# A two-layer decoder trunk: the up products of the experts as one product of 512 columns

## The chip, the core and the metric

One core of a Trainium2 chip runs the kernel, one launch for the whole trunk. The metric is the device time of that launch in microseconds (us), the median of several runs. Nothing is shared with other cores.

## The reference

The trunk has two layers. Each mixes 256 tokens of 1024 features with four token mixers; then layer 0 has a dense SwiGLU and layer 1 the part that matters here, eight SwiGLU experts of which each token takes its best two:

```python
def moe_swiglu(h, router_w, w1, w3, w2):
    logits = (xt @ router_w)
    top_v, top_i = lax.top_k(logits, TOP_K)
    gate = jax.nn.softmax(top_v, axis=-1)
    ...
    a = lax.ragged_dot(xs, w1, sizes)
    g = lax.ragged_dot(xs, w3, sizes)
    y = lax.ragged_dot(jax.nn.silu(a) * g, w2, sizes)
    y = y * gate.reshape(-1)[order][:, None]
    return jnp.zeros_like(xt).at[tok].add(y)
```

All is float32. w1 and w3 have 1024 rows and 2816 columns for each expert, w2 has 2816 rows and 1024 columns. Each expert's three matrices are read once, 277 MB in all.

## The kernel before, in words

**Products.** TensorE holds one operand, the stationary one (128 x 128, loaded by a weight load), and streams the other, the moving one, through it. A float32 product is made of three passes over halves that add up to the operands: `mm3` (line 642) issues xh times wh, xh times wl, and xl times wh into the same sums in PSUM. In the experts the tokens are stationary and the weights move.

**Weights.** `Stream` (line 138) loads weight pieces of 1 MB (128 partitions x 2048 columns) from a plan, in order, into a ring of slots; SyncE issues a load as soon as a slot is free. Each piece is split in two halves of 1024 columns: ScalarE writes the high part `wh` (a copy to the rounded type), VectorE the low part `wl` (raw minus wh), and the second half's split gives the slot back. The split halves live in a ring of four buffers (`NWH`, line 587), so a split can begin when the products of the half four places before it are done. `halves` (line 258) gives out a piece's halves and asks ahead of each for the splits of the next three.

**The experts' loop.** `moe` (line 1626) first routes, and gathers each expert's tokens into 128 slots. Then it goes over `pairs`, 8 experts x 11 chunks of 256 of the 2816 columns: 88 steps, in the loop from line 1841. Before the change a step i is, in the order of the code:

- `u`: 24 products of 256 columns (8 k tiles of the 1024 features x 3 passes) of the chunk of w1, by `up_half` (line 1810), into a PSUM bank of the pool `psm`, which has two; ScalarE's Silu of it goes to `es`;
- `at`: two transposes of the `es` of step i-1 (`flip_act`, line 1820), which ScalarE and VectorE split into `ath` (both halves under this name);
- `v`: the same 24 products of the chunk of w3, into the other bank; VectorE multiplies `es` by it;
- at some steps four products `scm` that scatter a finished expert's output to the tokens, or the turning of a one-hot (`rtm`);
- `y`: 12 products of 512 columns (`down`, line 1831) of step i-1 with its piece of w2, into two banks that sum over the expert's 11 chunks;
- at some steps four products `g` that gather tokens for the next two experts.

Six split halves are used in a step, two by each of u, v and y. For experts 3 and 7 the tokens lie in a tile `xe`, for the others in halves of `hh` and `hl`; the names in the rows say which.

**What sets the order.** Each engine runs its instructions in the order of the code. Splits come where `halves` asks for them, so a Silu's place among ScalarE's splits follows from where the code writes it. All instructions go through a helper, so that every row of the profile bears its line, L385; the tile names tell them apart.

Of the kernel before, what the change touches and what calls it, by code (L numbers as in the profile page):

```python
"""Two decoder layers (adaLN, four token mixers, SwiGLU / top-2 experts) in one launch.

Activations live feature-major ([feature on partitions, token on the free axis]) so that
weights are the stationary operand and no result of the dense layers needs a transpose.
Float32 products run as three float32r passes over exact two-way splits of both operands
(x = xh + xl, w = wh + wl): xh*wh + xl*wh + xh*wl.
"""
# [16 lines left out]
OP = mybir.AluOpType  # L24
# [18 lines left out]
# adaLN segments (layer, which) whose products run beside the mixers and the dense SwiGLU, and the  # L43
# least distance of their chunks
# [10 lines left out]
# products that nobody reads, at the places of the start where the tensor engine would wait  # L55
# [41 lines left out]
# the columns kept from the start on, those that the mixers use (the first of them at once), those of the experts  # L97
# [40 lines left out]
class Stream:  # L138
    """Weight chunks, loaded ahead in the plan's order through a ring of slots and split in two when
    they have come (the first two chunks' halves in turn); other chunks go on request through slots  # L140
    of their own."""
# [22 lines left out]
    def add_slots(self, pool, names, last=None):  # L164
        """last: key of the last chunk that may use these slots (None: no limit)."""
        for n in names:
            self.limit[n] = len(self.plan) if last is None else self.index[last]
            self.free.append((pool, n))
        self.issue()

    def add_halves(self, pool, names, last=None):
        """Buffers for split halves, used in turn."""
        for n in names:
            self.limit["wh" + n] = len(self.plan) if last is None else self.index[last]
            self.wring.appendleft((pool, n))
            self.look += 1

    def lane(self, name):
        """(chunks asked for, free slots) of a lane beside the ring."""
        return self.lanes.setdefault(name, (deque(), deque()))  # L180
# [5 lines left out]
    def move(self, lane, last=None):  # L186
        """A lane's slots, all free by now, go to the ring."""
# [39 lines left out]
    def ensure(self, upto):  # L227
        """Emit the splits of the pieces before this one."""
# [40 lines left out]
    def came(self, key):  # L269
        """When an unsplit chunk is there."""  # L270
# [10 lines left out]
class Clock:  # L281
    """A rough time per engine, kept as instructions are emitted: each starts when its engine is free
    and the operands (their boxes in a tile, the tile that had the buffer before) are."""
# [25 lines left out]
    def tile(self, ap):  # L309
        """The tile's accesses so far, {(box, engine, write): end}; those of the buffer's last owner  # L310
        count as one."""
# [14 lines left out]
    def free_at(self, tag, bufs):  # L326
        """When the next buffer of a tag is free."""
# [45 lines left out]
class Timed:  # L373
    """An engine whose instructions go through the clock."""
# [26 lines left out]
class Weave:  # L401
    """Emits the steps of background threads between the products of the main stream, so that no
    in-order engine gets a step whose inputs come late.

    A thread yields None after a step, "sync" before one that begins with a product of what the last
    step made, or a condition that gives False or the time it came true."""
# [65 lines left out]
class Ring:  # L472
    """Buffers handed out in turn: one is free again when all handed out before it are. The names in
    seq take theirs in that order, which keeps the threads from locking each other out."""
# [23 lines left out]
def trunk(ctx, tc, A):  # L498
# [28 lines left out]
    # ---------------------------------------------------------------- plan of the weight stream  # L527
# [12 lines left out]
    def add_item(it):  # L540
# [13 lines left out]
        elif k in ("e1", "e3"):  # L554
            add(it, A["moe_w1" if k == "e1" else "moe_w3"][0, l, it[2]])
# [22 lines left out]
    moe_items = with_lag([(("e1", e, j), ("e3", e, j)) for e, j in pairs], [("e2", e, j) for e, j in pairs])  # L578
# [11 lines left out]
    # ---------------------------------------------------------------- small loads  # L590
# [42 lines left out]
    # ---------------------------------------------------------------- helpers  # L633
# [8 lines left out]
    def mm3(out, ah, al, bh, bl, start, stop):  # L642
        """out += a^T b with a (stationary) and b (moving) both split.

        start clears the written marks of the whole bank, so where a bank holds several sums that
        grow side by side only its first product starts and only its last stops."""
# [4 lines left out]
    # ---------------------------------------------------------------- adaLN vectors  # L651
# [6 lines left out]
    def ada_mm(out, w, kk, start, stop):  # L658
        """One k tile of a segment: four column groups of 256, each on its own 32 rows."""
# [18 lines left out]
    def warm(n):  # L678
        """Products that nobody reads, where the tensor engine would wait: its clock halves when it idles."""
# [8 lines left out]
    def ada_cols(q, fill=lambda: warm(WARM[0])):  # L688
        """Two feature tiles of the two segments that the start waits for; fill puts other products where
        the tensor engine waits."""  # L690
# [18 lines left out]
    def ada_thread(ls, step):  # L709
        """The same products beside other work, a chunk per step of the clock: on DVE, but for the last sum."""  # L710
# [35 lines left out]
    class Gap:  # L746
        """A segment's products that fill the tensor engine's waits around a norm."""
# [30 lines left out]
    # ---------------------------------------------------------------- rope tables  # L778
# [25 lines left out]
    # ---------------------------------------------------------------- norm + modulation  # L804
# [3 lines left out]
    class Norm:  # L808
        """Sums of squares gathered as the features of x become final, then h = split(norm(x))."""
# [5 lines left out]
        def feed(self, dp):  # L815
            """Squares of feature tiles 2 dp, 2 dp + 1; those of the first two pairs are added up."""
# [14 lines left out]
        def feed_all(self):  # L831
            """The same for all of x at once, added up beforehand."""
# [13 lines left out]
        def stats(self, fill=lambda: None):  # L846
            """1 / rms on every partition, by token; fill puts other products where the tensor engine waits."""
# [20 lines left out]
        def tiles(self, ds, l, which, each=None):  # L868
            """Feature tiles ds of h; each(d): work that follows tile d."""
# [34 lines left out]
    # ---------------------------------------------------------------- dense products  # L904
    def feat_part(ps, w, h, ks):
        """ps[:, t*256 + tok] += (h W)[feature, tok] for a chunk's two feature tiles: k tiles ks of half h."""
# [7 lines left out]
    def tok_part(ps, w, h, ks, n=256):  # L914
        """ps[:, i*256 + c] += (h W)[token, column c] of token tile i."""
# [19 lines left out]
    def acc_chunk(key, ps4, xh, xl, first, then=None, mid=None):  # L935
        """ps4[d//2][:, (d%2)*256 + tok] += sum over the chunk's two k tiles (one per half).

        then: this is the last chunk, its pairs of feature tiles are finished one after the other and
        then(pair) takes them up."""
# [19 lines left out]
    # ---------------------------------------------------------------- mixer  # L959
    def mixer(l, mb, mp, pre):  # L960
        """pre: sums that are there already."""
# [22 lines left out]
        # --- projections  # L984
# [1096 lines left out]
```

## Time and profile before

| | us |
|---|---|
| median of 3 runs | 1587.01 |
| lowest, highest | 1582.55, 1589.59 |
| profiled execution, first to last instruction | 1583.4 |
| experts' steps in it, first u to last y | 780 to 1569 |

The profiled execution is one of the program's executions; no time is recorded for it but its span. In a row, `128x512 f32 x704` is the shape of an instruction's output and the count; "xcount" behind a duration in the chain or the timeline counts merged instructions. A duration in the order of time runs from an instruction's start to its end, and products overlap, so their spacing is read from starts. In the chain a piece lasts until the next begins. `u<-wh,hh` reads: tile u written from tiles wh and hh.

### The profile page before, as it was taken

How to read it: one execution, taken by the hardware profiler on the slowest of the kernel's cores; microseconds unless marked ns; L12 is line 12 of the kernel's file. 1: busy time of each engine (PE TensorE's matmuls, PEld its weight loads, DVE VectorE, ACT ScalarE, POOL GpSimd, SP SyncE). 2: the span in 40 equal slices, each digit the busy share in tenths (PEclk: the TensorE clock that was granted, in tenths of full speed). 3: DMA queues.
4: the chain of work that ended last, by engine and by line, in shares of the span. 5: the costliest groups of instructions: out<-in, count | busy, mean ns of one | idle time of the engine just before them, and what ended most of it. 6: DMA issues, size and time to landing. Idle time of an engine off the chain costs nothing.

```text
span 1583.4 us, 29781 instructions
## 1 busy us (share of the span) xinstructions
PE 1545.8 (98%) x12276; PEld 1458.3 (92%) x12276; DVE 1272.1 (80%) x1646; ACT 1032.9 (65%) x1452; POOL 56.2 (4%) x58
## 2 busy tenths in 40 slices
PE   8999998999999999999999999999999999999997
PEld 6998998899998999989889999999999999999996
DVE  4797897666656886776789988999889998898996
ACT  3546554544445546554677888878888788887884
POOL 0000013000001000121000000000000000000000
PEclk9999999999999999999999999999999999999999
DMA  9665657977633665539799999999999999999970
GB/s 369 226 231 179 232 193 261 368 266 248 232 115 132 236 233 168 186 134 380 272 341 366 350 331 358 352 344 364 338 359 356 360 349 330 359 349 362 358 261 29
DMA packets 84896, 446.28 MB, mean 282 GB/s; under 512 B 8080, under 2 KB 8464, under 8 KB 51344
## 3 DMA queue, kind: packets, MB, share of 16 engines
q1 hardware_dynamic: 84032, 443.71, 76.6%
q8 instruction: 98, 1.61, 0.4%
q10 hardware_dynamic: 720, 0.59, 0.1%
q14 instruction: 46, 0.38, 0.1%
HBM read 443.22 MB, written 1.05 MB: 281 GB/s over the span
## 4 chain that ended last, share of the span: by engine, by line
PE 80%; issue 13%; DVE 4%; ACT 1%; DMA 1%; POOL 0%; SPq 0%; DVEq 0%; POOLq 0%; ACTq 0%
PE u L385 16%; PE v L385 15%; PE y L385 15%; PE mg L385 11%; PE pt L385 7%; PE wo L385 2%; PE br L385 2%; PE at L385 1%; DVE wl L385 1%; PE g L385 1%; PE scm L385 1%; PE pcq L385 1%; PE ada L385 1%; PE pck L385 1%; PE oa L385 1%
## 5 line engine op out<-in xcount | busy, mean ns | idle before, releaser
L385 DVE TENSOR_TENSOR wl<-raw,wh 128x1024 fp32r<-128x1024 f32 x738 | 887.7, 1228 | 180.8 <-ACT wh L385 172.5
L385 ACT ACTIVATE wh<-raw 128x1024 fp32r<-128x1024 f32 x738 | 770.5, 1057 | 173.0 <-PE y L385 28.9
L385 PE MATMUL y<-wh,ath 128*128 128x512 f32 x704 | 233.9, 393 | 0.5 <-ACT ath L385 0.5
L385 PEld LDWEIGHTS y<-wh,ath 128*128 128x128 f32 x704 | 132.1, 188 | 27.1 <-ACT ath L385 0.7
L385 PE MATMUL v<-wh,hh 128*128 128x256 f32 x528 | 152.9, 290 | 0.0
L385 PE MATMUL mg<-hh,wh 128*128 128x256 f32 x512 | 147.6, 288 | 0.7 <-DVE brt L385 0.7
L385 PE MATMUL mg<-hh,wl 128*128 128x256 f32 x512 | 144.0, 281 | 4.1 <-DVE wl L385 4.1
L385 PE MATMUL u<-wh,hl 128*128 128x256 f32 x528 | 147.8, 280 | 0.0
L385 PE MATMUL v<-wl,hh 128*128 128x256 f32 x528 | 147.6, 279 | 0.0
L385 PE MATMUL u<-wh,hh 128*128 128x256 f32 x528 | 147.5, 279 | 0.0
L385 PE MATMUL v<-wh,hl 128*128 128x256 f32 x528 | 147.4, 279 | 0.0
L385 PE MATMUL u<-wl,hh 128*128 128x256 f32 x528 | 147.3, 279 | 0.0
L385 PE MATMUL mg<-hl,wh 128*128 128x256 f32 x512 | 143.3, 280 | 0.0
L385 PE MATMUL y<-wl,ath 128*128 128x512 f32 x352 | 137.8, 391 | 0.0
L385 PEld LDWEIGHTS mg<-hh,wl 128*128 128x128 f32 x512 | 97.2, 190 | 4.9 <-DVE wl L385 4.9
L385 PEld LDWEIGHTS u<-wl,hh 128*128 128x128 f32 x528 | 99.1, 188 | 1.8
L385 PEld LDWEIGHTS u<-wh,hh 128*128 128x128 f32 x528 | 98.9, 187 | 1.9
L385 PEld LDWEIGHTS mg<-hh,wh 128*128 128x128 f32 x512 | 97.3, 190 | 3.0 <-issue 2.0
L385 PEld LDWEIGHTS v<-wl,hh 128*128 128x128 f32 x528 | 99.4, 188 | 0.0
L385 PEld LDWEIGHTS v<-wh,hh 128*128 128x128 f32 x528 | 99.2, 188 | 0.0
L385 PEld LDWEIGHTS u<-wh,hl 128*128 128x128 f32 x528 | 99.1, 188 | 0.0
L385 PEld LDWEIGHTS v<-wh,hl 128*128 128x128 f32 x528 | 98.9, 187 | 0.0
(427 smaller groups left out, 3508.4 us busy)
## 6 DMA issues: line engine op xcount, KB each, us to landing
raw<-in_moe_w SPq DMA_DIRECT2D x263, 1024.0 KB, 5.7
raw<-in_w_in SPq DMA_DIRECT2D x54, 1024.0 KB, 5.1
aux<-in_w_ada SPq DMA_DIRECT2D x48, 1024.0 KB, 7.4
raw<-in_ffn_w SPq DMA_DIRECT2D x33, 1024.0 KB, 5.0
raw<-in_w_branch SPq DMA_DIRECT2D x8, 1024.0 KB, 5.0
raw<-in_w_out SPq DMA_DIRECT2D x8, 1024.0 KB, 5.0
raw<-in_w_in_tail SPq DMA_DIRECT2D x2, 576.0 KB, 3.9
xT<-in_x SPq DMA_DIRECT2D x1, 1024.0 KB, 5.4
```

Source lines behind the costliest of these rows:

```text
L385: r = f(*args, **kw)
```

## The change

The host puts the chunk of 256 columns of w1 and that of w3 side by side, for each k tile 512 columns; a piece of 1 MB then holds four k tiles of both in place of eight of one. One tile `uv` (a whole bank of 512 sums) takes both products: 24 products of 512 columns in two halves (`c` 0 and 1), with the transposes between them. The Silu is written after the second half and reads columns 0 to 255, VectorE's product reads columns 256 to 511. The branch for experts with over 128 tokens reads the new layout.

```diff
-        elif k in ("e1", "e3"):
-            add(it, A["moe_w1" if k == "e1" else "moe_w3"][0, l, it[2]])
+        elif k == "e13":
+            add(it, A["moe_w13"][0, l, it[2], it[3]])
...
-    moe_items = with_lag([(("e1", e, j), ("e3", e, j)) for e, j in pairs], [("e2", e, j) for e, j in pairs])
+    moe_items = with_lag([(("e13", e, j, 0), ("e13", e, j, 1)) for e, j in pairs], [("e2", e, j) for e, j in pairs])
...
-        def up_half(e, j, wi, ps):
+        def up_half(e, j, c, ps):
             Xh, Xl = X(e)
-            for h, (wh, wl) in enumerate(st.halves(("e1" if wi == 0 else "e3", e, j))):
-                whv = wh.rearrange("p (k n) -> p k n", k=4)
-                wlv = wl.rearrange("p (k n) -> p k n", k=4)
-                for k in range(4):
-                    kk = 4 * h + k
-                    mm3(ps[:, 0:256], Xh[:, kk, :], Xl[:, kk, :], whv[:, k, :], wlv[:, k, :],
+            for h, (wh, wl) in enumerate(st.halves(("e13", e, j, c))):
+                whv = wh.rearrange("p (k n) -> p k n", k=2)
+                wlv = wl.rearrange("p (k n) -> p k n", k=2)
+                for k in range(2):
+                    kk = 4 * c + 2 * h + k
+                    mm3(ps, Xh[:, kk, :], Xl[:, kk, :], whv[:, k, :], wlv[:, k, :],
                         start=(kk == 0), stop=(kk == KD - 1))
...
-            ps = pm(f"u{e}_{j}")
+            ps = pm(f"uv{e}_{j}")
             up_half(e, j, 0, ps)
+            if i:
+                flip_act(*pairs[i - 1])
+            up_half(e, j, 1, ps)
             s = sm.tile([P, 512], F32, name=f"es{e}_{j}", tag="sq", bufs=3)[:, 0:256]
             sc.activation(s, ps[:, 0:256], AF.Silu)
-            if i:
-                flip_act(*pairs[i - 1])
-            ps = pm(f"v{e}_{j}")
-            up_half(e, j, 1, ps)
-            dv.tensor_tensor(s, s, ps[:, 0:256], op=OP.mult)
+            dv.tensor_tensor(s, s, ps[:, 256:512], op=OP.mult)
...
-    a["moe_w1"] = cols(f["moe_w1"], NF)
-    a["moe_w3"] = cols(f["moe_w3"], NF)
+    up = np.stack([f[n].reshape(1, NE, 2, 4, P, NF, 256) for n in ("moe_w1", "moe_w3")], axis=6)
+    a["moe_w13"] = up.transpose(0, 1, 5, 2, 4, 3, 6, 7).reshape(1, NE, NF, 2, P, CH)
```

**TensorE, around the two transposes of step 9 of expert 0.** The number behind a name is the tile's own; `_9` and `_8` are chunks. Before:

```order
L385 MATMUL u_9_9870<-wh_9848,hh 128x256
L385 MATMUL u_9_9870<-wl_9849,hh 128x256
L385 MATMUL u_9_9870<-wh_9848,hl 128x256
L385 MATMUL at_8_9907<-cst,es_8_9804 128x128 x2
L385 MATMUL v_9_9913<-wh_9860,hh 128x256
L385 MATMUL v_9_9913<-wl_9861,hh 128x256
L385 MATMUL v_9_9913<-wh_9860,hl 128x256
```

After:

```order
L385 MATMUL uv_9_9645<-wh_9623,hh 128x512
L385 MATMUL uv_9_9645<-wl_9624,hh 128x512
L385 MATMUL uv_9_9645<-wh_9623,hl 128x512
L385 MATMUL at_8_9668<-cst,es_8_9620 128x128 x2
L385 MATMUL uv_9_9645<-wh_9635,hh 128x512
L385 MATMUL uv_9_9645<-wl_9636,hh 128x512
L385 MATMUL uv_9_9645<-wh_9635,hl 128x512
```

The transposes stay where they were, between two halves of the up products; on both sides of them stands now the same tile, with products of twice the columns, 12 in a half in place of 24.

**ScalarE, the same step: the Silu (`es`), the turned activation (`ath`) and the splits (`wh`).** Before:

```order
L385 ACTIVATE wh_9871<-raw_9448 128x1024
L385 ACTIVATE wh_9889<-raw_9471 128x1024
L385 ACTIVATE es_9_9905<-u_9_9870 128x256
L385 ACTIVATE ath_8_9910<-at_8_9907 128x256
L385 ACTIVATE wh_9914<-raw_9471 128x1024
L385 ACTIVATE wh_9932<-raw_9514 128x1024
L385 ACTIVATE wh_9949<-raw_9514 128x1024
```

After:

```order
L385 ACTIVATE wh_9646<-raw_9323 128x1024
L385 ACTIVATE wh_9658<-raw_9346 128x1024
L385 ACTIVATE ath_8_9671<-at_8_9668 128x256
L385 ACTIVATE wh_9674<-raw_9346 128x1024
L385 ACTIVATE wh_9686<-raw_9374 128x1024
L385 ACTIVATE es_9_9696<-uv_9_9645 128x256
L385 ACTIVATE wh_9699<-raw_9374 128x1024
```

The Silu has moved behind `ath` and behind two splits. VectorE's sequence of splits, `ath` and `es` is the same before and after.

## Rows read from the trace of the kernel before

**Rows 1.** The page: span, and busy time of each engine (part 1).

```profile
span 1583.4 us, 29781 instructions
...
PE 1545.8 (98%) x12276; PEld 1458.3 (92%) x12276; DVE 1272.1 (80%) x1646; ACT 1032.9 (65%) x1452; POOL 56.2 (4%) x58
```

**Rows 2.** Busy time by stretch, one expert each (experts 2 to 5); columns in the first line.

```profile
core 0: us, PE busy (x) PEld busy (x) DVE busy (x) ACT busy (x) POOL busy (x), PEclk, DMA share, GB/s
976.62:1074.18 97.56, 97.56 (x706) 91.99 (x705) 89.50 (x96) 79.72 (x99) 0.00 (x0) 1.00 0.96 353
1074.18:1173.98 99.80, 99.80 (x738) 94.38 (x737) 89.84 (x97) 83.18 (x115) 0.00 (x0) 1.00 0.95 351
1173.98:1271.54 97.56, 97.56 (x706) 91.98 (x705) 89.50 (x96) 79.73 (x99) 0.00 (x0) 1.00 0.96 356
1271.54:1372.45 100.91, 100.91 (x738) 95.48 (x736) 89.91 (x97) 83.13 (x115) 0.00 (x0) 1.00 0.94 344
```

**Rows 3.** Chain that ended last, 976.62 to 1372.45 us: shares of the stretch.

```profile
by line: PE u L385 31.2%; PE v L385 31.2%; PE y L385 30.8%; PE at L385 2.4%; PE g L385 1.9%; PE scm L385 1.9%; PE rtm L385 0.6%
```

**Rows 4.** The same chain, one step of expert 2: start, duration, what, products.

```profile
1045.63 2.73 PE y L385 x12
...
1057.02 2.83 PE u L385 x24
1059.85 0.22 PE at L385 x2
1060.07 2.83 PE v L385 x24
1062.90 2.78 PE y L385 x12
```

**Rows 5.** TensorE in order of time, expert 3: start, duration, line, what, tile, count.

```profile
1104.16 0.28 PE L385 MATMUL v<-wl,xe 128*128 128x256 f32 x1
...
1106.64 0.28 PE L385 MATMUL v<-wl,xe 128*128 128x256 f32 x1
...
1107.35 0.39 PE L385 MATMUL y<-wh,ath 128*128 128x512 f32 x1
...
1108.50 0.61 PE L385 MATMUL y<-wh,ath 128*128 128x512 f32 x2
...
1109.18 0.61 PE L385 MATMUL y<-wh,ath 128*128 128x512 f32 x2
...
1111.02 0.28 PE L385 MATMUL u<-wl,xe 128*128 128x256 f32 x1
...
1113.06 0.28 PE L385 MATMUL u<-wl,xe 128*128 128x256 f32 x1
```

**Rows 6.** Instructions by tile: es, whole stage of the experts.

```profile
L385 ACT ACTIVATE es<-u x88: 384/385/387, 784.1 to 1560.2; 128x256 f32<-128x256 f32 x88
```

**Rows 7.** Who waited for whom in the stage of the experts: total, times, longest.

```profile
ACT sam L385 <- PE scm L385: 22.4, 28, 0.8
```

**Rows 8.** ScalarE and VectorE in order of time, in the step of rows 4.

```profile
1059.88 0.39 ACT L385 ACTIVATE es<-u 128x256 f32<-128x256 f32 x1 [0.35 <-PE u L385]
...
1062.93 1.06 ACT L385 ACTIVATE wh<-raw 128x1024 fp32r<-128x1024 f32 x1 [0.35 <-PE v L385]
...
1063.80 0.41 DVE L385 TENSOR_TENSOR es<-es,v 128x256 f32<-128x256 f32 x1
1064.13 2.52 DVE L385 TENSOR_TENSOR wl<-raw,wh 128x1024 fp32r<-128x1024 f32 x2
```

**Rows 9.** SyncE's queue in the stage of the experts: whom its DMA issues waited for.

```profile
SPq L385 <- DVE wl L385: 648.3, 249, 11.3
```

**Rows 10.** Instructions by tile: raw, 1500 us to the end, splits and DMA issues.

```profile
L385 ACT ACTIVATE wh<-raw x45: 1055/1062/1068, 1499.6 to 1563.2; 128x1024 fp32r<-128x1024 f32 x45
L385 SPq DMA_DIRECT2D raw<-in_moe_w x11: 327/328/423, 1502.0 to 1529.3; - x11
...
DMA to landing us min/median/max: 4.8/5.9/6.8
```

More of the change, by code (lines that the diff above doesn't have):

```diff
@@ L1702, in moe @@
         dv.tensor_scalar(pos, msk, -1000.0, 1000.0, op0=OP.mult, op1=OP.add)
-        st.presplit(("e3", 0, 0), 2)
+        st.presplit(("e13", 0, 0, 1), 2)
         flipped(1)
@@ L1898, in moe @@
                     ws = []
-                    for key in ("moe_w1", "moe_w3"):
-                        wt = rpool.tile([P, CH], F32, name=f"x{key}{e}_{j}", tag="r0" if key == "moe_w1" else "r1")
-                        sy.dma_start(wt, A[key][0, e, j])
-                        ws.append(wt)
+                    for c in range(2):
+                        wt = rpool.tile([P, CH], F32, name=f"xw13{e}_{j}{c}", tag=f"r{c}")
+                        sy.dma_start(wt, A["moe_w13"][0, e, j, c])
+                        ws.append(wt.rearrange("p (k n) -> p k n", k=4))
                     w2t = fp.tile([P, CH], F32, name=f"xw2{e}_{j}", tag="f11")
@@ L1907, in moe @@
                         for wi in range(2):
-                            wx = ws[wi].rearrange("p (k n) -> p k n", k=KD)
                             for k in range(KD):
-                                pe.matmul(ps[:, wi * P:(wi + 1) * P], wx[:, k, t * P:(t + 1) * P], Xx[:, k, :],
+                                o = wi * 256 + t * P
+                                pe.matmul(ps[:, wi * P:(wi + 1) * P], ws[k // 4][:, k % 4, o:o + P], Xx[:, k, :],
                                           start=(k == 0), stop=(k == KD - 1))
@@ L1999, in trunk @@
             dbg(f"dbg_mix{l}")
-            st.presplit(("w1", 0, 0) if l == 0 else ("e1", 0, 0))
+            st.presplit(("w1", 0, 0) if l == 0 else ("e13", 0, 0, 0))
             nf.stats(lambda: g1.fill(FILL[2 * l][1]))
@@ L2003, in trunk @@
             if l == 1:
-                st.presplit(("e3", 0, 0), 1)
+                st.presplit(("e13", 0, 0, 1), 1)
             if l == 0:
```

## The prediction

> **What bounds the kernel now.** I read the page first: of a span of 1583.4 us TensorE's products cover 98% [rows 1]. A share over the whole program doesn't say what the experts' stage is worth, so the busy times by stretch come next, one expert at a time: in each of the four stretches the products fill all of it (97.56 of 97.56 us, for one), at a granted clock of 1.00, the full 2.4 GHz, while VectorE is busy for 89 to 92% of the stretch, ScalarE for 82 to 83%, and the DMA engines for 94 to 96% [rows 2]. Four resources are nearly full. Which of them ends last is said by the chain of waits: over these 44 steps it is TensorE's products and nothing else, 31.2% u, 31.2% v, 30.8% y, and no transfer, no split, no Silu [rows 3]. So TensorE sets the pace, and it never waits. What matters is how far apart its products start. "Mean ns of one" can't tell that, since products overlap; the differences of start times can.
>
> **The pace of a product.** The chain gives u and v 2.83 us for 24 products, 117.9 ns each, and y 2.73 or 2.78 us for 12 products of twice the columns, 227.5 or 231.7 ns [rows 4]. The order of time shows that each width has two paces. Products of 256 columns go on at 118.1 ns (21 of v between 1104.16 and 1106.64) or at 113.3 ns (18 of u between 1111.02 and 1113.06). Those of 512 begin near 230 ns (five from 1107.35 to 1108.50) and then settle at 226.7 ns (three to 1109.18), twice 113.3 [rows 5]. The narrow products run mostly at their slow pace, the wide ones settle within a few products. The means over four experts say the same: u and v are 62.4% of 395.83 us, 247.0 us for 44 steps, that is 5.614 us a step and 233.9 ns for the pair that one wide product replaces; y is 30.8%, 121.9 us, or 230.9 ns a product, its slow beginnings included [rows 2, 3].
>
> **The change, part by part.**
>
> *The products.* There are 88 steps (one Silu each) [rows 6], with 24 pairs in each: 2112 pairs become 2112 products of 512 columns, over the same weights, and as many weight loads fall away. If a wide product of uv runs at y's settled 226.7 ns, a pair saves 233.9 - 226.7 = 7.2 ns: 2112 x 7.2 = 15.2 us. Nothing hides this, since TensorE is the chain. The bounds: at the slowest plain piece of y, 231.7 ns, it is 2112 x 2.2 = 4.6 us. A price below 226.7 ns would take a pace that no run of y in the rows has. I take 226.7, because 24 wide products follow one another here, with 12 of y before and after, and the rows show that the pace settles within about five.
>
> Another account of a product's price: the Trainium skill, TensorE: Matmul & The Clock Gate (section "Wait — 56ns, not 53.3ns?"), gives the distance of warm products as the columns over 2.4 GHz plus about 2.5 ns. By it a pair would save 2112 x 2.5 = 5.3 us, an estimate from that page, and the median would become 1581.7. The trace doesn't agree with its figures: it shows 113.3 to 118.1 and 226.7 to 231.7 ns where they give 109.2 and 215.8.
>
> *Where it must settle again.* The two transposes of `at` stand between the halves of uv as they stood between u and v. Behind narrow products y's first five lose 5 x (230 - 226.7) = 17 ns [rows 5], in its slower beginnings 2.78 - 2.72 = 60 ns over 12 [rows 4]. Nearest to 12 of uv behind two transposes is the first; I take 25 ns a step, 88 x 25 = 2.2 us lost. In exchange y mostly follows wide products. Only in 28 steps does a scatter stand ahead of it [rows 7], and in 8 a one-hot's turn. In the other 52 y need not settle: 0 to 50 ns each (2.78 against 2.73) [rows 4], 0 to 2.6 us; I take 2.0.
>
> *ScalarE's order.* The Silu now waits for the end of both sums, and it stands two splits later in ScalarE's queue. Behind it wait the splits of the next weights, which TensorE reads through a ring of four. What it costs is read from the step of rows 4. The split that waits for the last half of v to be released starts at 1062.93; its low part is the first of the two at 1064.13, done by 1065.4. TensorE needs it for the second half of u, which comes after one y (2.78) and half of u (1.41) behind the end of v at 1062.90: at 1067.1 [rows 4, 8]. With the Silu right ahead of it the split starts some 0.4 us later; VectorE's product of the Silu (0.41) comes ahead of the low part in either order [rows 8]. Counted from the end of uv: Silu 0.4, split 1.06 more, low part 1.2 more, done at 2.7 us, needed at 2.73 + 1.36 = 4.1. That leaves 1.4 us, so I cost it at nothing. What hides it is y and the next half of uv; if that cover were gone, each us would cost 88 us.
>
> *VectorE* has the same 89.5 us of work in an expert of 97.56, which becomes about 95.7 [rows 2]: 94% in place of 92%. TensorE doesn't wait for it now, and on average 6 us an expert stay free; I take nothing, and leave a wait where its work bunches (an expert's scaled outputs) to the range.
>
> *The weights' stream.* The same 264 pieces of 1 MB come in the same sequence, cut otherwise. Its issues wait 648.3 us in all for VectorE to give back slots [rows 9], so TensorE paces the stream and not the other way. At 344 to 356 GB/s with 94 to 96% of the engines' time used [rows 2] there is little more to be had, so a faster TensorE will eat into the lead. The last piece is issued at 1529.3, lands within 6.8 us, by 1536.1, and its last half is split at 1563.2 [rows 10]: a lead of 27 us. Even a stream that speeds up not at all leaves 27 - 15 = 12 us. Cost: nothing.
>
> *Elsewhere* no engine's order moves ahead of the experts; the branch for experts of over 128 tokens is rewritten, and the rows after the last y hold none of it.
>
> **Sum:** 15.2 - 2.2 + 2.0 = 15.0 us. The profiled execution, 1583.4 us by its span, becomes 1568.4. It lies 3.6 us under the median of the runs shown, 1587.01, and against that median the forecast is **1572.0 us**, 0.95% faster. A measurement of this kernel can tell about 0.5%, 7.9 us, from no change.
>
> **The rivals.**
>
> 1. *The wide product is hardly cheaper than its pair*: uv doesn't settle and stays at the pace of y's slower piece, 231.7 ns against 233.9. For it: y has many such pieces, 2.78 us. Against it: pieces of 2.73 are there as well, and the slow ones are slow at their beginning [rows 4, 5]. Gain 4.6 us, time 1582.4, within 0.5%. Chance 0.13. The rule of the Trainium skill's TensorE: Matmul & The Clock Gate cited above, a small fixed price that is paid once in place of twice, would end near the same time.
>
> 2. *Another resource takes over*: VectorE at 94% of the new time, or the stream once its lead is gone. The gain is cut to between 0 and 4 us: 1583 to 1587. For it: rows 2 has both nearly full. Against it: the lead of 27 us and the 1.4 us worked out above. Chance 0.05.
>
> 3. *Slower: the Silu behind both sums holds up the splits.* As long as u had a bank of its own, its Silu ran beside v's products. Now it begins when uv ends, and the split that was next waits for it, so TensorE could come to wait at each second half of uv. It decides where the low part comes over 1.4 us later than I worked out; a step that waits 0.3 us costs 88 x 0.3 = 26.4 us, less the 15.0 gained: 1598.4. For it: in the rows the Silu and the splits do wait for TensorE, so ScalarE's order matters [rows 8]. Against it: the lead above. Chance 0.04. The Trainium skill's Perfetto Trace Analysis (section "Matmuls") speaks against the change in this way: independent groups of products should rotate through PSUM banks, so that one is read while the next is made; here two sums that were apart share a bank. Two banks still alternate from step to step, and whether that is enough no run here shows yet.
>
> That the change doesn't do what it says is excluded: TensorE's order shows one tile uv and products of 512 columns.
>
> **How the numbers follow.** The forecast's own case, gains of 9 to 18 us with 1569 to 1578 us, has 0.78. The range of 1566 to 1583 adds the first rival's end at its upper side and a little at the lower, since the runs shown lie up to 4.5 us under their median; it leaves out the slower cases. Faster by over 0.5% is the first case and a part of the first rival: 0.80. Within 0.5%: the rest of that rival and the second: 0.16. Slower: 0.04.
>
> **What would show it.** Right: uv in the chain at 2.72 to 2.76 us for 12 products, starts 226 to 227 ns apart from the sixth after `at`, a plain step of some 8.45 us in place of 8.66, TensorE without a wait, SyncE's waits for slots shorter, the lead of the last piece between 12 and 25 us. Wrong: products of uv at 230 ns or more throughout (first rival), a wait of TensorE for `wl` at the second half of uv (third), or a lead near zero (second).

## The result, and the profile after

The changed kernel takes 1576.5 us (median of 4 runs, 1573.86 to 1578.65), the kernel before beside it 1586.78 us (4 runs). The ratio is 0.9941 with a 95% interval of 0.9926 to 0.9955: 0.59% faster (by the interval 7.1 to 11.7 us less), where 0.95% was forecast. The profiled execution took 1573.86 us, its span is 1572.1.

The page's first part, which answers to [rows 1]: TensorE has 2112 products and as many weight loads fewer, and VectorE's work is the same.

```profile
span 1572.1 us, 25486 instructions
...
PE 1532.2 (97%) x10164; PEld 1352.0 (86%) x10164; DVE 1272.2 (81%) x1646; ACT 1037.2 (66%) x1452; POOL 56.2 (4%) x58
```

Busy time by stretch, experts 2 to 5 again, columns as in [rows 2]:

```profile
970.44:1066.17 95.73, 95.73 (x442) 78.75 (x440) 89.31 (x97) 80.30 (x99) 0.00 (x0) 1.00 0.96 363
1066.17:1166.62 100.45, 100.45 (x473) 82.67 (x472) 90.00 (x98) 83.75 (x115) 0.00 (x0) 1.00 0.93 346
1166.62:1262.34 95.72, 95.72 (x442) 78.75 (x441) 89.29 (x97) 80.29 (x99) 0.00 (x0) 1.00 0.96 362
1262.34:1361.85 99.51, 99.51 (x474) 82.57 (x472) 89.98 (x98) 83.74 (x115) 0.00 (x0) 1.00 0.94 349
```

Against [rows 2], experts 2 and 4 lose 1.83 and 1.84 us and expert 5 loses 1.40, but **expert 3 grows by 0.65 us**: 99.80 became 100.45. Experts 2, 4 and 5 have their tokens in `hh` and `hl`, expert 3 in `xe`. TensorE is still busy for all of each stretch at a granted clock of 1.00, and the chain of waits over the four is products alone, as in [rows 3]:

```profile
by line: PE uv L385 62.2%; PE y L385 31.0%; PE at L385 2.5%; PE g L385 1.9%; PE scm L385 1.9%; PE rtm L385 0.6%
```

Pieces of the chain, plain steps of expert 2 and the first of expert 3 (start, duration, what, products):

```profile
1043.90 2.77 PE uv L385 x12
1046.67 2.73 PE y L385 x12
1049.40 2.75 PE uv L385 x12
1052.15 0.22 PE at L385 x2
1052.37 2.77 PE uv L385 x12
...
1066.33 2.80 PE uv L385 x12
...
1069.35 2.80 PE uv L385 x12
```

A plain step with hh takes 8.47 us (1043.90 to 1052.37), 8.66 before; one with xe starts its halves with 2.80. In order of time, TensorE behind the transposes in expert 2, then in expert 3 (columns as in [rows 5]):

```profile
1061.14 0.39 PE L385 MATMUL uv<-wh,hl 128*128 128x512 f32 x1
...
1063.20 0.40 PE L385 MATMUL uv<-wh,hl 128*128 128x512 f32 x1
...
1077.98 0.40 PE L385 MATMUL uv<-wl,xe 128*128 128x512 f32 x1
...
1080.32 0.39 PE L385 MATMUL uv<-wh,xe 128*128 128x512 f32 x1
```

From 1061.14 to 1063.20 are 9 products, 228.9 ns apart; from 1077.98 to 1080.32 are 10, 234.0 ns apart. Neither settles at 226.7. The starts to the nanosecond show a cycle with hh and hl (226, 229, 232 ns, mean 229.0) and another with xe (231, 236 ns, mean 233.3).

The rest is as forecast. ScalarE's Silu waits for uv, VectorE's product follows (ScalarE and VectorE in order of time, the step of 1060.83):

```profile
1063.64 0.39 ACT L385 ACTIVATE es<-uv 128x256 f32<-128x256 f32 x1 [0.31 <-PE uv L385]
1063.92 2.15 ACT L385 ACTIVATE wh<-raw 128x1024 fp32r<-128x1024 f32 x2
1064.51 0.41 DVE L385 TENSOR_TENSOR es<-es,uv 128x256 f32<-128x256 f32 x1
1065.00 3.69 DVE L385 TENSOR_TENSOR wl<-raw,wh 128x1024 fp32r<-128x1024 f32 x3
```

The last row holds three low parts of 1.23 us; the first is done at 1066.2, 2.6 us behind the end of uv (1063.60), where 2.7 had been worked out.

TensorE's own waits in the experts' stage, all of them, stand once each and not in every step:

```profile
PE adat L385 <- DVE adarow L385: 1.8, 1, 1.8
PE y L385 <- ACT ath L385: 0.5, 1, 0.5
```

SyncE's issues wait 639.0 us where [rows 9] had 648.3; the last piece of weights is issued at 1517.1, lands within 7.6 us, and its last half is split at 1551.5, which answers to [rows 10]:

```profile
SPq L385 <- DVE wl L385: 639.0, 249, 10.1
```

```profile
L385 ACT ACTIVATE wh<-raw x37: 1052/1062/1066, 1500.0 to 1551.5; 128x1024 fp32r<-128x1024 f32 x37
...
L385 SPq DMA_DIRECT2D raw<-in_moe_w x7: 328/328/426, 1502.4 to 1517.1; - x7
...
DMA to landing us min/median/max: 5.7/7.0/7.6
```

**Where the time came from.** From the first up product to the start of the last y the stage took 789.23 us before (779.98 to 1569.21) and takes 780.18 (777.10 to 1557.27): 9.05 us less. The other 2.3 us of the spans' difference lie outside the stage: chiefly this execution reached it 2.9 us earlier, through code that the change leaves alone. Over the profiled executions below, one for each kernel, that arrival varies from 777.1 to 783.0, so the experiments are read from the stage. The one pair of kernels with the same paces agrees there to 0.2 us (789.23 and 789.07). Adding up, product by product, the time from one start to the next gives the shares (the one stall at `adat`, 2.1 and 2.2 us, is in both and left out):

| us | before | after | difference | forecast |
|---|---|---|---|---|
| up products with hh, hl (66 steps) | 378.2 | 369.2 | -9.0 | -9.75 |
| up products with xe (22 steps) | 123.9 | 125.1 | +1.1 | -3.25 |
| y | 243.5 | 242.4 | -1.1 | -2.0 |
| sum | 745.6 | 736.7 | -9.0 | -15.0 |

(The forecast's 15.2 and 2.2 are shared out over the steps: 24 x 7.2 - 25 = 148 ns a step.)

### The profile page after: what moved, and what is told of

Read it like the earlier page. It is cut to its first block, busy times and chain, and to the rows that moved or that the text cites. A ratio compares the mean times of both kernels' runs of the same rounds, so it can differ in the third digit from the quotient of the medians.

```text
span 1572.1 us, 25486 instructions
## 1 busy us (share of the span) xinstructions
PE 1532.2 (97%) x10164; PEld 1352.0 (86%) x10164; DVE 1272.2 (81%) x1646; ACT 1037.2 (66%) x1452; POOL 56.2 (4%) x58
## 4 chain that ended last, share of the span: by engine, by line
PE 79%; issue 15%; DVE 3%; DMA 1%; ACT 1%; POOL 1%; SPq 0%; DVEq 0%; POOLq 0%; ACTq 0%
PE uv L385 31%; PE y L385 15%; PE mg L385 11%; PE pt L385 7%; PE br L385 2%; PE at L385 1%; PE wo L385 1%; PE g L385 1%; PE scm L385 1%; DVE wl L385 1%; PE pcq L385 1%; PE ada L385 1%; PE pck L385 1%; PE oa L385 1%; DMA aux<-in_nsa_ck_w 0%
## 5 line engine op out<-in xcount | busy, mean ns | idle before, releaser
L385 PE MATMUL uv<-wh,hh 128*128 128x512 f32 x528 | 212.9, 403 | 0.0
L385 PE MATMUL uv<-wh,hl 128*128 128x512 f32 x528 | 207.0, 392 | 0.0
L385 PE MATMUL uv<-wl,hh 128*128 128x512 f32 x528 | 206.7, 392 | 0.0
L385 PE MATMUL uv<-wh,xe 128*128 128x512 f32 x352 | 119.1, 401 | 0.0
L385 PEld LDWEIGHTS uv<-wh,hl 128*128 128x128 f32 x528 | 99.1, 188 | 22.5
L385 PEld LDWEIGHTS uv<-wh,hh 128*128 128x128 f32 x528 | 99.2, 188 | 18.5
L385 PEld LDWEIGHTS uv<-wl,hh 128*128 128x128 f32 x528 | 99.4, 188 | 18.0
L385 PEld LDWEIGHTS mg<-hl,wh 128*128 128x128 f32 x512 | 96.7, 189 | 1.0 <-issue 1.0
L385 PE MATMUL pt<-wh,hh 128*128 128x256 f32 (+1 forms) x320 | 90.3, 282 | 0.0
L385 PE MATMUL pt<-wl,hh 128*128 128x256 f32 (+1 forms) x320 | 89.2, 279 | 0.0
```

Source lines behind the costliest of these rows:

```text
L385: r = f(*args, **kw)
```

## The experiments

**1. Is it the width, or all that came with it?** The changed kernel with its layout, bank and order, but each product of 512 columns issued as two of 256:

```diff
-                    mm3(ps, Xh[:, kk, :], Xl[:, kk, :], whv[:, k, :], wlv[:, k, :],
-                        start=(kk == 0), stop=(kk == KD - 1))
+                    for n in range(2):
+                        o = slice(n * 256, (n + 1) * 256)
+                        mm3(ps[:, o], Xh[:, kk, :], Xl[:, kk, :], whv[:, k, o], wlv[:, k, o],
+                            start=(kk == 0 and n == 0), stop=(kk == KD - 1 and n == 1))
```

> The changed kernel with each product of 512 columns issued as two of 256, first the columns of w1, then those of w3; layout, bank and order of the engines stay. Theory 1 (the width alone gives the gain in pace): the products go back to 117 to 118 ns each, a pair to 234 to 236 ns, so the experts' stage from the first up product to the last y is some 6 us longer than the changed kernel's 780.2 us; what the first step gained (2.1 us) and nothing else stays, so 786 to 788 us against 789.2 before. Theory 2 (the gain comes from the order of the Silu or from the shared bank): the stage stays at 780 to 782 us.

Measured: ratio to before 1.0001 (0.9987 to 1.0016), stage 789.07 us. In experts 2 and 3 by stretch TensorE has the very times of [rows 2]:

```profile
977.29:1074.85 97.56, 97.56 (x705) 91.99 (x704) 89.62 (x97) 80.27 (x99) 0.00 (x0) 1.00 0.96 357
1074.85:1174.65 99.80, 99.80 (x737) 94.38 (x736) 89.79 (x98) 83.78 (x115) 0.00 (x0) 1.00 0.94 348
```

At these places of the tiles the whole gain goes with the width, and with the weight loads that fall away with it. Layout, shared bank and the Silu's place together give and take nothing. What this expectation kept for the first step was a misreading: that stall is TensorE's wait at `adat`, which every kernel has.

**2. The Silu's place alone.** The kernel before, with only the Silu moved behind v:

```diff
-            s = sm.tile([P, 512], F32, name=f"es{e}_{j}", tag="sq", bufs=3)[:, 0:256]
-            sc.activation(s, ps[:, 0:256], AF.Silu)
+            pu = ps
...
             up_half(e, j, 1, ps)
+            s = sm.tile([P, 512], F32, name=f"es{e}_{j}", tag="sq", bufs=3)[:, 0:256]
+            sc.activation(s, pu[:, 0:256], AF.Silu)
```

> The kernel before with the Silu alone moved behind the products of v, so that ScalarE has the order of the changed kernel, with two banks and products of 256 columns. Theory 1: the products keep their pace, and only the wait of 2.1 us in the first step, where the Silu's table load stood ahead of a split, goes: stage 787.0 us against 789.2, the same time within what can be measured. Rival (the third of the prediction): TensorE waits for wl at each second half, 88 waits of 0.1 us or more, and the stage is over 797 us.

Measured: ratio 1.0017 (1.0004 to 1.0029), stage 790.88 us, 1.65 more than before. TensorE's waits hold one new line, once, in the first steps:

```profile
PE u L385 <- ACT es L385: 1.4, 1, 1.4
```

That Silu is the first, which stands behind a table load of 1.28 us (from 787.04). No wait comes back step by step, so the slower rival's mechanism is not there: 88 steps with a later Silu cost 1.65 us in all. The 787.0 us expected rested on the misreading told under 1.

**3. The price of a product by itself.** Groups of 48 products, each with its own weight load, the stationary tiles placed 0, 64, ... 448 bytes past a multiple of 512 and the moving ones at 0 (`wa` to `wh` with 512 columns, `na` to `nh` with 256), and four groups with both moved alike (`ma` to `md`):

```diff
+GROUPS += [("w" + "abcdefgh"[i], 512, 64 * i, 0) for i in range(8)]
+GROUPS += [("n" + "abcdefgh"[i], 256, 64 * i, 0) for i in range(8)]
+GROUPS += [("m" + "abcd"[i], 512, o, o) for i, o in enumerate((64, 192, 320, 384))]
```

> Products alone, without the trunk (the output is x, and nothing of the reference is computed): groups of 48 in the pattern of three passes, one after the other on TensorE, with no other engine at work. The stationary tiles start 0, 64, ... 448 bytes off a multiple of 512 from where the moving ones start (groups wa to wh with 512 columns, na to nh with 256); groups ma to md move both by the same bytes. Theory A (the pace that a product settles at depends on where its stationary tile lies relative to the moving one; in the trunk 0 bytes for y, 192 for hh and hl, 320 for xe): wa and ma to md settle at 226.7 ns, wd (192) near 229.0, wf (320) near 233.4; na to nh differ as well, between 113.3 and 118. Rival B (the pace comes from what stands before, or from the other engines' reads and writes): all wide groups settle at 226.7 and all narrow ones at one pace.

TensorE in order of time (start, duration, line, what, tile, count); a group's pace is the distance to the next group's start over 48:

```profile
24.32 11.04 PE L47 MATMUL wa<-mv,st 128*128 128x512 f32 x48
35.20 11.36 PE L47 MATMUL wb<-mv,st 128*128 128x512 f32 x48
46.39 11.32 PE L47 MATMUL wc<-mv,st 128*128 128x512 f32 x48
57.55 11.16 PE L47 MATMUL wd<-mv,st 128*128 128x512 f32 x48
68.55 11.06 PE L47 MATMUL we<-mv,st 128*128 128x512 f32 x48
...
112.80 5.92 PE L47 MATMUL na<-mv,st 128*128 128x256 f32 x48
118.56 5.61 PE L47 MATMUL nb<-mv,st 128*128 128x256 f32 x48
124.01 5.85 PE L47 MATMUL nc<-mv,st 128*128 128x256 f32 x48
```

wa: 10.88 us for 48, 226.7 ns; wb: 11.19, 233.1; wd: 11.00, 229.2; na: 5.76, 120.0; nb: 5.45, 113.5. Settled, over the last 24 of each group:

| distance, stationary less moving, modulo 256 bytes | 512 columns | 256 columns |
|---|---|---|
| 0 | 226.7 ns | 120.0 ns |
| 64 | 233.3 | 113.3 (nb), 117.8 (nf) |
| 128 | 232.7 | 118.8 |
| 192 | 228.9 | 117.8 |

All four groups with both operands moved alike settle at 226.7, so for wide products it is the distance that counts and not the place. For narrow ones the distance alone does not fix the pace: at 64 there are two. By the addresses in the compiled kernels, which no trace holds, `ath` lies at distance 0 from the weights, `hh` and `hl` at 192, `xe` at 64; the cycles of 226, 229, 232 ns (wd) and of 231, 236 ns (wb) are those of the kernel. The bench ran once.

**4. All distances to 0.** The changed kernel with the experts' stationary tiles moved by 64 bytes (hh, hl) and 192 bytes (xe):

```diff
-    NSLOT, NWH, NWX, NX = 3, 4, (0, 0), (4, 5)
+    NSLOT, NWH, NWX, NX = 3, 4, (0, 0), (4, 4)
...
-    hh = cpool.tile([P, KD, S], F32R, name="hh")
-    hl = cpool.tile([P, KD, S], F32R, name="hl")
+    ht = cpool.tile([P, 2 * KD * S + 64], F32R, name="hh")
+    rows = lambda o: ht[:, o:o + KD * S].rearrange("p (k s) -> p k s", k=KD)
+    hh, hl = rows(0), rows(KD * S)
+    hx, lx = rows(16), rows(KD * S + 16)
...
+        xet = mb.tile([P, 2 * KD * SLOTS + 64], F32R, name="xe", tag="merged")
+        xe = xet[:, 48:48 + 2 * KD * SLOTS].rearrange("p (a k s) -> p a k s", a=2, k=KD)
...
-            return hh[:, :, c], hl[:, :, c]
+            return hx[:, :, c], lx[:, :, c]
```

> The changed kernel with only the places of the experts' stationary tiles moved in SBUF: for the experts' stage the halves of h begin 64 bytes further and xe 192 bytes further, so that every stationary column block lies a multiple of 256 bytes from the weights it is multiplied with, as ath does for the second product and as the group wa did in the bench. The room is found by giving the last weight ring four slots instead of five. Theory A (the pace of wide products is set by the distance between the stationary and the moving operand, modulo 256 bytes): all 2112 uv products settle at 226.7 ns, with hh and hl as with xe; the stage shrinks by 1584 x 2.3 ns + 528 x 6.6 ns = 7.1 us, from 780.2 to about 773 us, and the kernel takes about 1569.4 us. Rival B (the pace belongs to the buffers or to the order of the products and not to their distance): 229.0 and 233.3 ns stay, and the stage stays at 780 us. Rival C (the weight stream with one slot less becomes the bound): the pace is 226.7 ns but TensorE now waits for splits, and the stage stays above 776 us.

Measured: ratio to before 0.9921 (0.9907 to 0.9934); stage 777.12 us, 3.06 less than the changed kernel's, where 7.1 were expected. Behind the transposes, in order of time:

```profile
905.71 0.40 PE L385 MATMUL uv<-wl,hh 128*128 128x512 f32 x1
...
907.79 0.39 PE L385 MATMUL uv<-wl,hh 128*128 128x512 f32 x1
908.02 0.39 PE L385 MATMUL uv<-wh,hh 128*128 128x512 f32 x1
908.24 0.28 PE L385 MATMUL scm<-ohs,yhm 128*128 128x256 f32 x1
```

Nine products from 905.71 to 907.79 stand 231.1 ns apart, the last two 230 and 220 to the rows' hundredths (227 and 226 by the starts in nanoseconds): 226.7 is reached, but only by the last two of twelve. Where uv follows y at once it runs at 226.7 from the first product. So the settled paces are right (rival B falls), no wait for splits came (rival C falls), and a chain of 12 behind the transposes is too short for its pace.

**5 to 7. Other distances, both widths.** The same edit with `rows(32)`, `rows(KD * S + 32)` and xe unmoved, so that all lie at 64, in the changed kernel (5) and in the kernel before (6); and the edit of 4 in the kernel before (7).

> The same kernel as the one before it with other distances: the halves of h begin 128 bytes further and xe stays, so that hh, hl and xe all lie 64 bytes (modulo 256) from the weights, as xe does in the changed kernel and as the group wb did in the bench. Theory A: all uv products settle in the cycle of 231 and 236 ns (mean 233.3); the stage grows by 1584 x (233.3 - 229.0) = 6.8 us to about 787.0 us, the kernel takes about 1583 us, and nearly all of the change's gain is gone. Rival B: 229.0 ns stays with hh and hl, stage 780 us.

> The kernel before, its products of 256 columns kept, with the distances of the kernel before this one in the list (64 bytes modulo 256 for hh, hl and xe), and four slots in the last weight ring. In the bench narrow products at this distance ran at 113.3 ns in one group and 117.8 in another, and xe in the kernel before shows both. Theory A (distance decides for narrow products too, at 64 bytes with two paces): the 3168 products with hh and hl come down from 117.7 ns to between 113.3 and 117.8, at a half and half mix 115.6: the stage shrinks by about 6.7 us to 782.5 us (775.3 if all run at 113.3, 789 if none does). Rival B (the gain belongs to the width alone and cannot be had with narrow products): 117.7 ns stays, stage 789.2 us.

> The kernel before, its products of 256 columns kept, with the distances that are a multiple of 256 bytes, and four slots in the last weight ring. In the bench narrow products at this distance ran at 120.0 ns, the slowest pace of all narrow groups, while wide ones were fastest there. Theory A: u and v settle at 120.0 ns with hh, hl and xe: the stage grows by 3168 x 2.3 ns + 1056 x 3.5 ns = 11 us to about 800 us, the kernel takes about 1597 us. Rival B: 117.7 ns stays, stage 789 us. Against this kernel the changed widths at the same place would be worth 2112 x (2 x 120.0 - 226.7) = 28 us.

Experts 2 and 3 by stretch, runs 5, 6 and 7 in turn:

```profile
975.47:1072.34 96.87, 96.87 (x442) 79.02 (x441) 89.38 (x97) 80.28 (x99) 0.00 (x0) 1.00 0.95 358
1072.34:1172.81 100.47, 100.47 (x473) 82.75 (x472) 89.99 (x98) 83.74 (x115) 0.00 (x0) 1.00 0.92 345
```

```profile
973.23:1069.58 96.35, 96.35 (x706) 90.97 (x704) 89.07 (x96) 79.67 (x99) 0.00 (x0) 1.00 0.96 361
1069.58:1169.37 99.79, 99.79 (x737) 94.39 (x736) 89.86 (x97) 83.14 (x115) 0.00 (x0) 1.00 0.96 348
```

```profile
981.60:1079.94 98.34, 98.34 (x706) 92.94 (x704) 89.54 (x96) 79.73 (x99) 0.00 (x0) 1.00 0.94 354
1079.94:1182.06 102.12, 102.12 (x738) 96.72 (x736) 90.00 (x97) 83.17 (x115) 0.00 (x0) 1.00 0.94 340
```

| stage, us (ratio of the kernel to before) | 256 columns | 512 columns | the width is worth |
|---|---|---|---|
| hh, hl at 192, xe at 64 (as given) | 789.23 (1) | 780.18 (0.9941) | 9.05 |
| all at 64 | 782.06 (0.9956, 0.9939 to 0.9972) | 786.62 (0.9973, 0.9957 to 0.9989) | -4.6 |
| all at 0 | 799.00 (1.0057, 1.0041 to 1.0072) | 777.12 (0.9921, 0.9907 to 0.9934) | 21.9 |

All three came within 1 us of what theory A expected (787.0, 782.5, 800), and rival B falls in each. The 28 us that the width was to be worth at 0 came out at 21.9, since the wide chains do not settle there (run 4). In run 6 a plain step's u goes on at 118 ns and v, behind the transposes, at 113.3, and u behind a gather runs at 113.3 too, exactly as xe did before (a step's up products take 5.64 us with hh, 5.63 with xe). **The same merge is worth 22 us, 9 us, or less than nothing, by where the stationary tile lies.** And moving the tiles alone (run 6) took 7.2 us off the stage, without any merge.

**8, 9. A longer chain.** In the aligned kernel (8) and in the changed kernel (9) the transposes go ahead of all 24 products:

```diff
+            if i:
+                flip_act(*pairs[i - 1])
             ps = pm(f"uv{e}_{j}")
             up_half(e, j, 0, ps)
-            if i:
-                flip_act(*pairs[i - 1])
             up_half(e, j, 1, ps)
```

> The aligned kernel, with the transposes of the previous pair's activations put ahead of the 24 uv products instead of between the two twelves. In the aligned kernel each chain of 12 begins with 235, 233, 236, 224, 231, 236, 228, 233, 231 ns and reaches 226.7 ns only at its tenth product, so the stage came down to 777.1 us and not to 773. Theory (a chain has to run for some ten products until it reaches the pace that its distance gives, and every interruption begins it anew): with one chain of 24 the second half runs at 226.7 ns; a step's uv products take 314 + 2087 + 14 x 226.7 = 5575 ns instead of 2770 + 2853 = 5623 ns, 48 ns less, 4.2 us in 88 steps: stage about 773 us, kernel about 1570 us. Rival (the slow pace is not a settling but belongs to the place or order, as to the first half of a chunk): the second twelve also run at 231 ns and the stage stays at 777 us. Rival (the transposes now wait for VectorE's product of the previous pair): TensorE waits at at, and the stage grows.

> The changed kernel with its distances as they are (192 bytes for hh and hl, 64 for xe), and the transposes put ahead of the 24 uv products. There the chain goes into its cycle of 226, 229 and 232 ns (with xe 231 and 236) within a few products, so that little is to be had from a longer one. Theory: a step's uv products take about 312 + 23 x 229 = 5579 ns instead of 2763 + 2834 = 5597 ns, 18 ns less in 66 steps and nothing in the 22 with xe: about 1.2 us, stage 779 us, kernel within 0.2% of the changed kernel. Rival (the place of the transposes alone is worth what it brings in the aligned kernel): stage 776 us.

Measured: ratios 0.9940 (0.9924 to 0.9957) and 0.9973 (0.9961 to 0.9986); stages 780.28 and 784.17 us, 3.2 and 4.0 more than without the edit. Both are misses. Run 8, TensorE's waits from 780 to 800 us, two stretches of it (columns as in [rows 2]), and TensorE in order of time:

```profile
PE at L385 <- DVE es L385: 1.9, 1, 1.9
```

```profile
786.00:790.00 4.00, 2.06 (x11) 1.43 (x10) 2.81 (x3) 2.79 (x4) 0.00 (x0) 1.00 0.43 137
790.00:794.00 4.00, 4.00 (x13) 3.08 (x12) 2.88 (x3) 2.33 (x3) 0.00 (x0) 0.60 0.54 156
```

```profile
790.99 1.05 PE L385 MATMUL uv<-wh,hh 128*128 128x512 f32 x2
...
793.55 0.93 PE L385 MATMUL uv<-wh,hh 128*128 128x512 f32 x2
```

In the first step no y stands between uv and the next transposes, so these waited for VectorE's product. Behind that the granted clock was 0.60 from 790 to 794, and from 790.99 to 793.55 six products stood 426.7 ns apart: 512 columns at the lower of the clock's two levels, 1.2 GHz. (The Trainium skill, TensorE: Matmul & The Clock Gate, section "Back-to-back issue gap", gives the columns over 1.2 GHz as the spacing at that level. By it I estimate 426.7 ns, and this trace agrees.) By the starts in nanoseconds the wait and the slow products cost 3.7 us together. Run 9 has the same event (a granted clock of 0.57 from 786 to 790), at 3.7 us too.

Taken off, run 8 would stand at 776.5 and run 9 at 780.4, so the event is not the whole of either miss. In run 8 the longer chain did settle: in 84 of the 88 steps its second twelve run at 226 and 227 ns. It gained less than the 48 ns a step that was expected, since in plain steps uv already followed y unbroken: those take 8.43 us in runs 4 and 8 alike, and only steps with a gather fell (from 9.45 to 9.40 where they have a scatter too). In run 9 the 1.2 us that were expected did not come: nothing is left of a gain.

**10. The longer chain without its first step.**

```diff
-            if i:
+            if i > 1:
                 flip_act(*pairs[i - 1])
             ps = pm(f"uv{e}_{j}")
             up_half(e, j, 0, ps)
+            if i == 1:
+                flip_act(*pairs[0])
             up_half(e, j, 1, ps)
```

> The aligned kernel with one chain of 24, but in the very first step the transposes stay between the two twelves. In the run without this the first transposes, put behind no other product, waited 1.95 us for VectorE's product, and then nine uv products ran 314 to 427 ns apart at a granted clock of 0.60 in that stretch: 2.3 + 9 x 180 ns = 3.7 to 4.0 us more than in the aligned kernel, which is all that it lost. Theory: neither the wait nor the slow products come, the steps with a gather keep 9.41 us against 9.45 in the aligned kernel, and the stage is 780.3 - 3.8 = 776.5 us, 0.6 us under the aligned kernel's 777.1; the kernel about 0.992 of the kernel before. Rival (the place of the transposes costs time in other steps as well): stage 778 us or more.

Measured: stage 776.52 us, ratio 0.9928 (0.9915 to 0.9941), median 1572.96 us against 1584.25. Experts 2 and 3:

```profile
974.09:1069.57 95.48, 95.48 (x444) 78.81 (x442) 89.62 (x96) 80.29 (x99) 0.00 (x0) 1.00 0.95 359
1069.57:1169.01 99.44, 99.44 (x476) 82.91 (x474) 90.58 (x97) 83.74 (x115) 0.00 (x0) 1.00 0.95 347
```

As expected: the loss of run 8 was that one event. Runs 4 and 10 are the best versions, with stages 3.1 and 3.7 us under the changed kernel's. Their ratios' intervals overlap with the change's, so over the whole kernel only the stage shows that they are ahead.

## Why the prediction was right, and where its sum was wrong

*Right: TensorE is the chain, and nothing takes over.* It never waits in a steady step; a plain step with hh took 8.47 us, where 8.45 was named; VectorE's work of 89.3 us now fills 93% of an expert's 95.73, close to the 94% forecast. *The stream* kept up better than I allowed: the lead of the last piece is 26.8 us (1551.5 less 1524.7), as good as the 27 before and outside my 12 to 25. Its issues waited for slots 9.3 us less, about the time the stage lost: it sped up with TensorE. *The Silu's place* cost nothing in the change, as worked out; alone it cost 1.65 us, once (run 2).

*The step that failed* is the price of a wide product: "I take 226.7, because 24 wide products follow one another here, with 12 of y before and after, and the rows show that the pace settles within about five." The rows show that y settles at 226.7. They don't show that uv would, and it does not: the value belongs to the distance between the two operands, and y's stationary operand lies elsewhere than uv's. With xe the starts stand 231 to 236 ns apart throughout, which the prediction had named as a sign of the first rival. The term of 15.2 us, less the 2.2 for settling, measured 7.9 (9.0 less 1.1).

- *With xe* the term had the wrong sign, and this is 4.4 of the 6.0 us that the sum was off. The mean of 233.9 ns a pair over four experts hid that pairs with xe were cheap. Of the 44 chains of 24 narrow products with xe, 26 settled at 113.3 ns: 18 of v, and the 8 of u behind a gather. Of the 132 with hh and hl four did; all others ran at 117.8. Pieces of the chain before, expert 3, from a plain step and from steps with a gather:

```profile
1082.88 2.83 PE u L385 x24
...
1085.93 2.74 PE v L385 x24
...
1101.26 2.73 PE u L385 x24
...
1104.21 2.83 PE v L385 x24
```

  [rows 2] had it: expert 3 at 99.80 us against 100.91 for expert 5 with as many products. [rows 5] could not tell, since they are all of expert 3 and both narrow paces read `xe` there: v at 118.1 and u at 113.3, both from steps with a gather. I averaged over the two paces without asking where each belongs. Merged, xe has the dearest wide pace, 233.3 ns.
- *With hh and hl* 9.0 us came of 9.75. The settled pace is 229.0 in place of 226.7, 1584 x 2.3 = 3.6 us dearer. What made up for most of it: uv goes into its cycle at once, so that the 25 ns a step for settling weren't paid (66 x 25 = 1.65 us), and pairs with hh had been dearer than the mean I started from (5.73 us a step, 5.63 with xe).
- *y*, taken at 2.0 us, gave 1.1.

*Luck.* That the forecast held hung on where the tiles happen to lie, which the prediction did not weigh: with all of them at 64 the same change makes the stage 4.6 us longer (runs 6 and 5). And with hh and hl the total came out near the forecast because the errors offset each other.

*The rivals.* The first (uv stays near y's slow pace, 231.7 ns) had the size of the pace about right, but named the wrong reason: uv settles, at a pace of its own. The stage lost 9.05 us, and with other distances 21.9 or gained 4.6, so by these runs no fixed price for a product describes it. The rule of the Trainium skill's TensorE: Matmul & The Clock Gate (section "Wait — 56ns, not 53.3ns?") that was weighed, some 2.5 ns once in place of twice, would give 5.3 us by estimate; these runs do not agree with it. The third (a later Silu holds up the splits) fell in run 2. Two sums in one bank with two banks in turn cost TensorE no wait here, and run 1, with the shared bank and narrow products, took what the kernel before took. The Trainium skill's Perfetto Trace Analysis (section "Matmuls") advises rotating banks between independent groups of products. These runs show nothing lost by the two sums' sharing one.

*Left open.* What in the chip makes the distance count, why narrow products have two paces at one distance (at 64 bytes hh in run 6 has both, as xe has, and at 192 four chains ran at 113.3), whether for narrow products, too, the distance alone counts and not the place, and why a chain at distance 0 needs five products to settle behind one neighbour and nine behind another, no run here shows.

## What to carry to other kernels

Ask of every row with two paces what differs between its instructions, the tiles' names and what stands ahead of them, and look beyond one expert, before taking a mean or the better of the two. Where TensorE is the chain, measure the pace of a stream of products for the distance modulo 256 bytes between its stationary and its moving tiles: padding by 64 or 192 bytes was worth 3 us on top of the merge here, 7.2 us in the kernel before by another distance, and it decides whether merging pays at all. A settled pace is only worth what a chain is long enough to reach, and reordering to lengthen it must be looked at in the first step, where what covers it isn't there yet.

## What was not expected of the hardware

- The spacing of products with a weight load each, at a granted clock of 1.00, depends on the distance of their operands: 226.7 to 233.3 ns at 512 columns and 113.3 to 120.0 at 256, and the order of the distances is another for either width (run 3). At 256 columns and 64 bytes both 113.3 and 117.8 occur: u had the lower one behind a gather and the higher one behind y, in every step with xe before and with hh in run 6.
- At its best a pair of narrow products costs what a wide one does: 2 x 113.3 against 226.7 ns.
- One wait of 1.9 us early in the stage was followed by products 427 ns apart (runs 8 and 9); in run 8 the wait of 1.8 us at `adat` some 18 us later was not: the granted clock is 1.00 from 797.4 to 808 and from 808 to 820.
